# Short-sequence attention: Q and K turned by VectorE 32x32 blocks instead of by TensorE, scores as two accumulating 32-row matmuls, one exp per 2048 columns

## The chip, the cores and the metric

The kernel runs on one core of a Trainium2 chip. The metric is device microseconds for one execution; lower is better. A profiled execution additionally leaves a trace: every instruction of each engine (PE is TensorE's matmuls, PEld its weight loads, DVE is VectorE, ACT ScalarE, POOL GpSimd, SP SyncE) and every DMA packet.

## The reference

For each of 32 x 12 = 384 heads, with 128 positions and a head dimension of 64, all float32 in and out:

```python
def reference(q, k, v):                       # each (32, 12, 128, 64)
    scale = 1.0 / np.sqrt(q.shape[-1])
    scores = scale * np.matmul(q, k.transpose(0, 1, 3, 2))
    scores_max = np.max(scores, axis=-1, keepdims=True)
    attn = np.exp(scores - scores_max)
    attn = attn / (np.sum(attn, axis=-1, keepdims=True) + 1e-8)
    return np.matmul(attn, v).astype(np.float32)
```

The inputs are small (0.1 times a normal draw), so both kernels take the exponential without subtracting the maximum.

## The kernel before

**Layout.** The position index of a head is split as `s = g*4 + t` (32 groups `g` of `T = 4` consecutive positions). One partition row holds one `(head, g)`, so four heads (`A = 4`, index `a`) fill the 128 partitions and make one block; a row then holds 4 x 64 consecutive floats of memory. There are 96 blocks. A chunk is `CB = 4` blocks (16 heads), and there are `NCH = 24` chunks.

**Loads.** All 72 loads (`q_bf`, `k_bf`, `v_bf` of each chunk, L69) are issued by GpSimd at the start, ahead of all compute, and turn float32 into bfloat16 on the way. Every chunk has buffers of its own (`pin`, 24 of them), so no load waits for compute.

**Compute** goes by pairs of blocks (48 pairs, two to a chunk), in three stages that are one pair apart; the order is written out by hand (`manual_schedule`), and each engine works through its list in that order:

- `stage_a`: 16 TensorE transposes of Q and K into `t_ps` (L87), one VectorE copy of the result into `qkt` (L91); 16 matmuls with a slice of the identity that gather V's rows by head into `v_ps` (L98), one ScalarE copy into one of four `v2s` tiles (L103). A column of ones stands beside V there, so that the last product also gives the row sums.
- `stage_b`: 8 matmuls K·Qᵀ (contraction over 64 rows) into `s_ps` (L111), and one exponential of 1024 columns into `attn` (L117).
- `stage_c`: 32 matmuls attn·V into `o_ps` (L130), a reciprocal of the row sums (L140) and a multiplication (L141) on VectorE into `o_sb`; after the second pair of a chunk SyncE stores the chunk (L144).

PSUM is full: `t_ps` and `v_ps` have one buffer each, `s_ps` two, and `o_ps` one. Every TensorE matmul or transpose is two instructions for the engine, a weight load and a matmul; a pair of blocks has 16 + 16 + 8 + 32 = 72 of them, hence 144 instructions, and a chunk 288.

Of the kernel before, what the change touches and what calls it, by code (L numbers as in the profile page):

```python
# [9 lines left out]
@with_exitstack  # L10
def kernel(
    ctx: ExitStack,
    tc: tile.TileContext,
    q: bass.AP,
    k: bass.AP,
    v: bass.AP,
    out: bass.AP,
):


    nc = tc.nc
    f32 = mybir.dt.float32
    bf16 = mybir.dt.bfloat16

    B, H, S, D = q.shape
    assert S == 128 and D == 64
    scale = 1.0 / (D ** 0.5)
    T = 4
    A = 4
    G = S // T  # L30
    NBLK = B * H // A
    CB = 4
    NCH = NBLK // CB
    NG = NBLK // 2
    GPC = CB // 2

    def blocks(x):
        return x.rearrange("b h (g t) d -> (b h g) (t d)", t=T).rearrange(
            "(n p) x -> p n x", p=128)

    qr, kr, vr, orr = blocks(q), blocks(k), blocks(v), blocks(out)

    singles = ctx.enter_context(tc.tile_pool(name="singles", bufs=1))
    pin = ctx.enter_context(tc.tile_pool(name="pin", bufs=NCH))
    pt = ctx.enter_context(tc.tile_pool(name="pt", bufs=3))
    pa = ctx.enter_context(tc.tile_pool(name="pa", bufs=3))
    po = ctx.enter_context(tc.tile_pool(name="po", bufs=4))
    ps_t = ctx.enter_context(tc.tile_pool(name="ps_t", bufs=1, space=bass.MemoryType.PSUM))
    ps_v = ctx.enter_context(tc.tile_pool(name="ps_v", bufs=1, space=bass.MemoryType.PSUM))
    ps_s = ctx.enter_context(tc.tile_pool(name="ps_s", bufs=2, space=bass.MemoryType.PSUM))  # L50
    ps_o = ctx.enter_context(tc.tile_pool(name="ps_o", bufs=1, space=bass.MemoryType.PSUM))

    ident = singles.tile([128, 128], bf16)
    make_identity(nc, ident)
    NV2 = 4
    v2s = []
    for i in range(NV2):
        v2 = singles.tile([128, A, 2, D + 1], bf16, name=f"v2_{i}")
        nc.vector.memset(v2[:, :, :, D:D + 1], 1.0)  # L59
        v2s.append(v2)  # L60

    chunks = {}

    def load(c):
        sl = slice(c * CB, (c + 1) * CB)
        tiles = []
        for src, tag in ((qr, "q_bf"), (kr, "k_bf"), (vr, "v_bf")):
            x = pin.tile([128, CB, T, D], bf16, tag=tag, name=tag)
            nc.gpsimd.dma_start(out=x, in_=src[:, sl, :].rearrange("p n (t d) -> p n t d", t=T))  # L69
            tiles.append(x)  # L70
        chunks[c] = tiles

    for c in range(NCH):
        load(c)

    with tc.manual_schedule():
        qkts, attns, osbs = {}, {}, {}

        def stage_a(i):
            c, r = divmod(i, GPC)  # L80
            q_bf, k_bf, v_bf = chunks[c]
            bs = slice(2 * r, 2 * r + 2)
            t_ps = ps_t.tile([128, T, 2, 128], bf16, tag="t_ps", name="t_ps")
            for t in range(T):
                for j, x in enumerate((q_bf, k_bf)):
                    for b in range(2):
                        nc.tensor.transpose(  # L87
                            t_ps[b * D:(b + 1) * D, t, j, :], x[:, 2 * r + b, t, :], ident,
                            tile_position=(0, b * D))
            qkt = pt.tile([128, 2, A, T, G], bf16, tag="qkt", name="qkt")  # L90
            nc.vector.tensor_copy(  # L91
                qkt.rearrange("p j a t g -> p t (j a) g"),
                t_ps.rearrange("p t j (a g) -> p t (j a) g", a=A))
            qkts[i] = qkt
            v_ps = ps_v.tile([128, A, 2, D], f32, tag="v_ps", name="v_ps")
            for a in range(A):
                for t in range(T):
                    nc.tensor.matmul(  # L98
                        v_ps[t * G:(t + 1) * G, a, :, :],
                        lhsT=ident[:, a * G:(a + 1) * G],  # L100
                        rhs=v_bf[:, bs, t, :],
                        start=True, stop=True, tile_position=(0, t * G))
            nc.scalar.copy(v2s[i % NV2][:, :, :, :D], v_ps)  # L103

        def stage_b(i):
            qkt = qkts.pop(i)
            s_ps = ps_s.tile([128, 2, A, 128], f32, tag="s_ps", name="s_ps")
            for a in range(A):
                for j in range(2):
                    pr = slice(j * D, (j + 1) * D)  # L110
                    nc.tensor.matmul(  # L111
                        s_ps[:, j, a, :],
                        lhsT=qkt[pr, 1, a].rearrange("p t g -> p (t g)"),
                        rhs=qkt[pr, 0, a].rearrange("p t g -> p (t g)"),
                        start=True, stop=True)
            attn = pa.tile([128, 2, A, 128], bf16, tag="attn", name="attn")
            nc.scalar.activation(out=attn, in_=s_ps, func=mybir.ActivationFunctionType.Exp,  # L117
                                 bias=0.0, scale=scale)
            attns[i] = attn

        def stage_c(i):
            c, r = divmod(i, GPC)
            attn = attns.pop(i)
            v2 = v2s[i % NV2]
            o_ps = ps_o.tile([128, 2, 512], f32, tag="o_ps", name="o_ps")
            for j in range(2):
                ov = o_ps[:, j, :T * (D + 1)].rearrange("p (t e) -> p t e", t=T)
                for t in range(T):
                    for a in range(A):
                        nc.tensor.matmul(  # L130
                            ov[a * G:(a + 1) * G, t, :],
                            lhsT=attn[:, j, a, t * G:(t + 1) * G],
                            rhs=v2[:, a, j, :],
                            start=True, stop=True, tile_position=(0, a * G))
            ov = o_ps[:, :, :T * (D + 1)].rearrange("p j (t e) -> p j t e", t=T)
            if r == 0:
                osbs[c] = po.tile([128, CB, T, D], f32, tag="o_sb", name="o_sb")
            o_sb = osbs[c]
            recip = pa.tile([128, 2, T], f32, tag="recip", name="recip")
            nc.vector.reciprocal(recip, ov[:, :, :, D])  # L140
            nc.vector.tensor_mul(o_sb[:, 2 * r:2 * r + 2], ov[:, :, :, :D],  # L141
                                 recip.to_broadcast([128, 2, T, D]))
            if r == GPC - 1:
                nc.sync.dma_start(  # L144
                    out=orr[:, c * CB:(c + 1) * CB, :],
                    in_=o_sb.rearrange("p n t d -> p n (t d)"))
                osbs.pop(c)

        for s in range(NG + 2):
            if s < NG:  # L150
                stage_a(s)
            if 0 <= s - 1 < NG:
                stage_b(s - 1)
            if 0 <= s - 2 < NG:
                stage_c(s - 2)


# [28 lines left out]
```

## Time and profile before

| | |
|---|---|
| median of 3 runs | 168.92 us (168.44 to 169.7) |
| the profiled execution | 168.79 us, of which the trace spans 167.0 us |
| PE busy / PEld busy | 108.6 / 80.4 us |
| VectorE busy / ScalarE busy / GpSimd busy | 74.4 / 76.2 / 54.1 us |
| mean granted TensorE clock | 0.759 of full speed |
| TensorE instructions | 3456 matmuls and 3456 weight loads |
| bytes | 37.75 MB read from HBM, 12.58 MB written |

No engine is busy for much over two thirds of the span, so the busy shares alone don't tell what sets the time. The span has two stages that are read apart: while inputs are being loaded, and after that.

### The profile page before, as it was taken

What the parts mean: (1) busy time and instruction counts of PE and PEld (TensorE: products, weight loads), DVE (VectorE), ACT (ScalarE), POOL (GpSimd) and SP (SyncE); (2) the same over time, 40 slices, a digit from 0 to 9 for tenths busy, and PEclk for the clock granted to TensorE, in tenths of its full rate; (3) what the DMA queues carried; (4) which work ended last, traced back from release to release, by engine and by line L of the source; (5) the groups of instructions that cost most, each with busy time, mean ns of one, the idle gap of its engine ahead of it and who ended that gap; (6) DMA issues with size and microseconds to landing.
All of it is one profiled execution on the core that took longest, in us unless ns stands there. A gap on an engine that the chain in (4) does not pass through costs nothing.

```text
span 167.0 us, 7438 instructions
## 1 busy us (share of the span) xinstructions
PE 108.6 (65%) x3456; PEld 80.4 (48%) x3456; DVE 74.4 (45%) x148; ACT 76.2 (46%) x97; POOL 54.1 (32%) x78
## 2 busy tenths in 40 slices
PE   0279619559558747686796576675595688878730
PEld 0256517446346435454574454454473566656520
DVE  0035515444334453333373351373433377767640
ACT  3027533336253353371544272570362676767730
POOL 7955535343433534444433533534000000000000
PEclk9999995876955895555567855696555899999985
DMA  3999999999999999999999999999999133333333
GB/s 45 141 195 198 192 226 202 237 209 231 231 208 241 197 242 237 201 241 198 223 218 242 218 222 240 197 244 222 214 235 219 46 129 134 129 129 129 129 129 126
DMA packets 50718, 31.93 MB, mean 191 GB/s; under 512 B 1536, under 2 KB 50688, under 8 KB 50688
## 3 DMA queue, kind: packets, MB, share of 16 engines
q0 software_dynamic: 38016, 18.88, 84.3%
q1 hardware_dynamic: 12672, 12.58, 25.3%
q8 instruction: 27, 0.44, 1.0%
q14 instruction: 3, 0.02, 0.0%
HBM read 37.75 MB, written 12.58 MB: 301 GB/s over the span
## 4 chain that ended last, share of the span: by engine, by line
PE 38%; DMA 38%; issue 16%; DVE 3%; POOL 3%; POOLq 0%
DMA k_bf<-in_k_dram 16%; PE t_ps L87 13%; DMA v_bf<-in_v_dram 13%; PE o_ps L130 10%; DMA q_bf<-in_q_dram 9%; PE v_ps L98 8%; PE s_ps L111 7%; DVE o_sb L141 2%; POOL q_bf L69 1%; POOL k_bf L69 1%; DVE qkt L91 1%; DVE recip L140 1%; POOL v_bf L69 0%; POOL ident masks.py:199 0%; POOL ident masks.py:197 0%
## 5 line engine op out<-in xcount | busy, mean ns | idle before, releaser
L103 ACT CAST v<-v_ps 128x512 bf16<-128x512 f32 x48 | 28.2, 587 | 76.9 <-PE v_ps L98 76.7
L117 ACT ACTIVATE attn<-s_ps 128x1024 bf16<-128x1024 f32 x48 | 49.1, 1026 | 6.2 <-PE s_ps L111 6.2
L87 PE MATMUL t_ps<-ident,q_bf 128*64 128x128 bf16 x384 | 38.7, 274 | 7.6 <-DMA q_bf<-in_q_dram 5.1
L87 PE MATMUL t_ps<-ident,k_bf 128*64 128x128 bf16 x384 | 38.4, 271 | 8.0 <-issue 5.9
L130 PE MATMUL o_ps<-v,attn 128*32 128x65 bf16 x1536 | 27.9, 218 | 22.5 <-issue 20.6
L91 DVE COPY qkt<-t_ps 128x1024 bf16<-128x1024 bf16 x48 | 33.0, 687 | 20.6 <-PE t_ps L87 19.7
L140 DVE RECIPROCAL recip<-o_ps 128x8 f32<-128x8 f32 x48 | 10.0, 208 | 65.4 <-PE o_ps L130 64.7
L87 PEld LDWEIGHTS <-q_bf 128*64 128x64 bf16 x384 | 27.1, 139 | 16.5 <-issue 8.1
L130 PEld LDWEIGHTS <-attn 128*32 128x32 bf16 x1536 | 19.4, 110 | 31.3 <-issue 27.9
L141 DVE TENSOR_TENSOR o_sb<-o_ps,recip 128x512 f32<-128x512 f32 x48 | 33.2, 691 | 1.9 <-DVE recip L140 0.3
L98 PE MATMUL v_ps<-v_bf,ident 128*32 128x128 bf16 x768 | 25.3, 263 | 9.5 <-issue 6.4
L87 PEld LDWEIGHTS <-k_bf 128*64 128x64 bf16 x384 | 28.2, 143 | 3.7 <-DMA k_bf<-in_k_dram 2.3
L111 PE MATMUL s_ps<-qkt 64*128 64x128 bf16 x384 | 24.5, 260 | 6.0 <-issue 6.0
L69 POOL DMA_DIRECT2D k_bf<-in_k_dram x24 | 17.9, 746 | 22.2 <-DMA v_bf<-in_v_dram 22.2
L69 POOL DMA_DIRECT2D q_bf<-in_q_dram x24 | 18.0, 752 | 21.2 <-DMA k_bf<-in_k_dram 20.9
L69 POOL DMA_DIRECT2D v_bf<-in_v_dram x24 | 17.9, 745 | 19.0 <-DMA q_bf<-in_q_dram 19.0
L98 PEld LDWEIGHTS <-ident 128*32 128x32 bf16 x768 | 14.2, 111 | 16.7 <-issue 12.0
L111 PEld LDWEIGHTS <-qkt 64*128 64x128 bf16 x384 | 13.7, 110 | 13.5 <-issue 10.8
L103 ACT ACT_TABLE_LOAD x1 | 1.3, 1283 | 0.7 <-PEq L170 0.7
L59 DVE MEMSET v<- 128x8 bf16 x4 | 0.2, 65 | 0.8 <-PEq L170 0.8
masks.py:199 POOL TENSOR_SCALAR_AFFINE_SELECT ident<-ident 128x128 bf16<-128x128 bf16 x1 | 0.3, 304 | 0.1
masks.py:197 POOL MEMSET ident<- 128x128 bf16 x1 | 0.2, 204 | 0.3 <-POOLq L170 0.3
(4 smaller groups left out, 0.4 us busy)
## 6 DMA issues: line engine op xcount, KB each, us to landing
out_dram<-o_sb SPq DMA_DIRECT2D x24, 512.0 KB, 7.6
q_bf<-in_q_dram POOLq DMA_DIRECT2D x24, 256.0 KB, 13.8
k_bf<-in_k_dram POOLq DMA_DIRECT2D x24, 256.0 KB, 13.9
v_bf<-in_v_dram POOLq DMA_DIRECT2D x24, 256.0 KB, 14.0
```

What stands on the lines that cost most here:

```text
L59: nc.vector.memset(v2[:, :, :, D:D + 1], 1.0)
L69: nc.gpsimd.dma_start(out=x, in_=src[:, sl, :].rearrange("p n (t d) -> p n t d", t=T))
L87: nc.tensor.transpose(t_ps[b * D:(b + 1) * D, t, j, :], x[:, 2 * r + b, t, :], ident, tile_position=(0, b * D))
L91: nc.vector.tensor_copy(qkt.rearrange("p j a t g -> p t (j a) g"), t_ps.rearrange("p t j (a g) -> p t (j a) g", a=A))
L98: nc.tensor.matmul(v_ps[t * G:(t + 1) * G, a, :, :], lhsT=ident[:, a * G:(a + 1) * G], rhs=v_bf[:, bs, t, :], start=True, stop=True, tile_ ...
L103: nc.scalar.copy(v2s[i % NV2][:, :, :, :D], v_ps)
L111: nc.tensor.matmul(s_ps[:, j, a, :], lhsT=qkt[pr, 1, a].rearrange("p t g -> p (t g)"), rhs=qkt[pr, 0, a].rearrange("p t g -> p (t g)"), st ...
L117: nc.scalar.activation(out=attn, in_=s_ps, func=mybir.ActivationFunctionType.Exp, bias=0.0, scale=scale)
L130: nc.tensor.matmul(ov[a * G:(a + 1) * G, t, :], lhsT=attn[:, j, a, t * G:(t + 1) * G], rhs=v2[:, a, j, :], start=True, stop=True, tile_pos ...
L140: nc.vector.reciprocal(recip, ov[:, :, :, D])
L141: nc.vector.tensor_mul(o_sb[:, 2 * r:2 * r + 2], ov[:, :, :, :D], recip.to_broadcast([128, 2, T, D]))
```

## The change

TensorE no longer transposes. A VectorE 32x32-block transpose (`turn`, L78) goes from the loaded tile in SBUF to a `qt` or `kt` tile in SBUF, 1024 columns at a time, one for Q and one for K of each chunk. It transposes inside groups of 32 partitions, so head `a` comes to lie on partitions `32a` to `32a+31`, with the 64 features as two groups of 32 (`J = 2`). The scores of a head are thus two matmuls with 32 contraction rows each, accumulated in PSUM, and each head uses a row group of the array of its own (`tile_position=(a * 32, 0)`, L101). The work goes by chunks of four blocks: V's matmuls have 256 columns (L89), the exponential 2048 (L107), V's copy 1024 (L92). PSUM: `s_ps` takes four banks, `v_ps` two, `o_ps` two, one buffer each. `v2s` has three tiles. The loads, the output product, its two VectorE instructions and the store are as before, now in `outputs` and `finish`.

```diff
-    ps_t = ctx.enter_context(tc.tile_pool(name="ps_t", bufs=1, space=bass.MemoryType.PSUM))
+    ps_s = ctx.enter_context(tc.tile_pool(name="ps_s", bufs=1, space=bass.MemoryType.PSUM))
     ps_v = ctx.enter_context(tc.tile_pool(name="ps_v", bufs=1, space=bass.MemoryType.PSUM))
-    ps_s = ctx.enter_context(tc.tile_pool(name="ps_s", bufs=2, space=bass.MemoryType.PSUM))
     ps_o = ctx.enter_context(tc.tile_pool(name="ps_o", bufs=1, space=bass.MemoryType.PSUM))
...
+        def turn(c, which):
+
+            x = chunks[c][which]
+            xt = pt.tile([128, J, CB, T, G], bf16, tag="qk"[which] + "t", name="qk"[which] + "t")
+            nc.vector.transpose(
+                xt.rearrange("p j n t g -> p (n t) j g"),
+                x.rearrange("p n t (j e) -> p (n t) j e", j=J))
+            qts[c, which] = xt
+
+        def values(c):
+
+            v_bf = chunks[c][2]
+            v_ps = ps_v.tile([128, A, CB, D], f32, tag="v_ps", name="v_ps")
             for a in range(A):
                 for t in range(T):
                     nc.tensor.matmul(
-                        v_ps[t * G:(t + 1) * G, a, :, :],
-                        lhsT=ident[:, a * G:(a + 1) * G],
-                        rhs=v_bf[:, bs, t, :],
-                        start=True, stop=True, tile_position=(0, t * G))
-            nc.scalar.copy(v2s[i % NV2][:, :, :, :D], v_ps)
+                        v_ps[t * G:(t + 1) * G, a], lhsT=ident[:, a * G:(a + 1) * G],
+                        rhs=v_bf[:, :, t, :], start=True, stop=True, tile_position=(0, t * G))
+            nc.scalar.copy(v2s[c % NV2][:, :, :, :D], v_ps)
...
+        def scores(c):
+            qt, kt = qts.pop((c, 0)), qts.pop((c, 1))
+            s_ps = ps_s.tile([128, A, CB, 128], f32, tag="s_ps", name="s_ps")
+            for n in range(CB):
+                for j in range(J):
+                    for a in range(A):
+                        pr = slice(a * 32, (a + 1) * 32)
+                        nc.tensor.matmul(
+                            s_ps[:, a, n, :],
+                            lhsT=kt[pr, j, n].rearrange("p t g -> p (t g)"),
+                            rhs=qt[pr, j, n].rearrange("p t g -> p (t g)"),
+                            start=(j == 0), stop=(j == J - 1), tile_position=(a * 32, 0))
+            attn = pa.tile([128, A, CB, 128], bf16, tag="attn", name="attn")
             nc.scalar.activation(out=attn, in_=s_ps, func=mybir.ActivationFunctionType.Exp,
                                  bias=0.0, scale=scale)
-            attns[i] = attn
+            attns[c] = attn
...
+        turn(0, 0)
+        turn(0, 1)
+        values(0)
+        for s in range(NCH + 1):
+            c, p, f = s, s - 1, s + 1
+            if c < NCH:
+                scores(c)
+            o0 = outputs(p, 0) if p >= 0 else None
+            if f < NCH:
+                turn(f, 0)
+            if o0 is not None:
+                finish(p, 0, o0)
+            if f < NCH:
+                values(f)
+                turn(f, 1)
+            if p >= 0:
+                finish(p, 1, outputs(p, 1))
```

How the instructions stand shows best on VectorE. Before, in the steady state, one pair of blocks (`t_ps`, `o_ps` are PSUM tiles; a name behind "waits" is the semaphore, of TensorE, of VectorE itself, or of a store that still reads `o_sb`):

```order
L91 COPY qkt<-t_ps 128x4x8x32 [waits PE_49]
L140 RECIPROCAL recip<-o_ps 128x8 [waits PE_49]
L141 TENSOR_TENSOR o_sb<-o_ps,recip 128x512 [waits DVE_49]
L91 COPY qkt<-t_ps 128x4x8x32 [waits PE_49]
L140 RECIPROCAL recip<-o_ps 128x8 [waits PE_49]
L141 TENSOR_TENSOR o_sb<-o_ps,recip 128x512 [waits DMAHW1_49,DVE_49]
```

A chunk had two such copies out of PSUM, each behind TensorE. Now the same stretch of one chunk on VectorE, where DMASW names the semaphore of a load:

```order
L78 STREAM_TRANSPOSE qt<-q_bf 128x16x2x32 [waits DMASW2_49]
L131 RECIPROCAL recip<-o_ps 128x8 [waits PE_49]
L132 TENSOR_TENSOR o_sb<-o_ps,recip 128x512 [waits DMAHW0_49,DVE_49]
L78 STREAM_TRANSPOSE kt<-k_bf 128x16x2x32 [waits DMASW3_49]
L131 RECIPROCAL recip<-o_ps 128x8 [waits PE_49]
L132 TENSOR_TENSOR o_sb<-o_ps,recip 128x512 [waits DMAHW1_49,DVE_49]
```

VectorE itself now waits for loads: each transpose is for the chunk two after the one whose two finishing instructions stand behind it.

On TensorE, the list of before at the turn from one pair of blocks to the next, where a run of the same pair of rows is cut:

```order
L130 LDWEIGHTS attn [waits DVE_49,Activation_49]
L130 MATMUL o_ps<-v_3_93,attn 32x65 [waits PE_49]
...
L87 LDWEIGHTS q_bf [waits DMASW1_49]
L87 MATMUL t_ps<-ident,q_bf 64x128 [waits DVE_49]
...
L87 LDWEIGHTS k_bf [waits DMASW2_49]
...
L98 LDWEIGHTS ident [waits DMASW3_49]
L98 MATMUL v_ps<-v_bf,ident 32x128 [waits Activation_49]
```

And TensorE's list now, over one chunk:

```order
L101 LDWEIGHTS kt [waits DVE_49]
L101 MATMUL s_ps<-qt,kt 128x128 [waits Activation_49]
...
L120 LDWEIGHTS attn [waits DVE_49]
L120 MATMUL o_ps<-v_0_84,attn 32x65 [waits PE_49]
...
L89 LDWEIGHTS ident [waits DMASW1_49]
L89 MATMUL v_ps<-v_bf,ident 32x256 [waits Activation_49]
...
L120 LDWEIGHTS attn [waits DVE_49]
L120 MATMUL o_ps<-v_0_84,attn 32x65 [waits PE_49]
```

TensorE waits for a load at V's matmuls alone; a chunk has 32 score matmuls, 32 output matmuls, 16 for V and again 32 output matmuls, 224 instructions with their weight loads, where there were 288.

## Rows read from the trace of the kernel before

**Rows 1.** The page: span, and three of its rows in 40 slices of 4.175 us.

```profile
span 167.0 us, 7438 instructions
...
PEclk9999995876955895555567855696555899999985
DMA  3999999999999999999999999999999133333333
GB/s 45 141 195 198 192 226 202 237 209 231 231 208 241 197 242 237 201 241 198 223 218 242 218 222 240 197 244 222 214 235 219 46 129 134 129 129 129 129 129 126
```

**Rows 2.** Waits: engine, line, waited for: us in total, times, longest us.

```profile
PEld L130 <- issue: 27.9, 36, 4.0
...
PE o_ps L130 <- issue: 20.6, 13, 3.8
```

**Rows 3.** Windows from gap to gap on TensorE while loading: busy us (instructions), clock.

```profile
44.30:50.70 6.40, 3.96 (x127) 2.85 (x127) 2.29 (x4) 3.12 (x4) 2.93 (x4) 0.60 1.37 222
...
63.60:70.00 6.40, 4.80 (x127) 3.62 (x127) 3.18 (x6) 2.63 (x3) 2.22 (x3) 0.50 1.36 226
...
sum 63.90, PE 44.19 PEld 32.80 DVE 28.12 ACT 27.08 POOL 26.56; mean PE 4.42 PEld 3.28 DVE 2.81 ACT 2.71 POOL 2.66
```

**Rows 4.** The same after the loads, two windows of five.

```profile
144.10:147.90 3.80, 2.89 (x127) 2.11 (x127) 2.21 (x5) 2.95 (x4) 0.00 (x0) 1.00 0.37 125
147.90:151.85 3.95, 3.32 (x127) 2.52 (x127) 2.99 (x6) 2.53 (x5) 0.00 (x0) 1.00 0.31 104
```

**Rows 5.** DMA queues over the whole span: packets, MB, share of 16 engines.

```profile
q0 software_dynamic: 38016, 18.88, 84.3%
q1 hardware_dynamic: 12672, 12.58, 25.3%
q8 instruction: 27, 0.44, 1.0%
```

**Rows 6.** DMA queue of the loads, 0 to 10 us.

```profile
q0 software_dynamic: 2196, 1.09, 88.9%
```

**Rows 7.** The same, 10 to 20 us, when no store moves yet.

```profile
q0 software_dynamic: 3900, 1.94, 144.0%
```

**Rows 8.** Loads and stores, 20 to 120 us.

```profile
q0 software_dynamic: 29458, 14.63, 108.5%
q1 hardware_dynamic: 7392, 7.34, 26.6%
```

**Rows 9.** Stores issued from 130 us on: how many, KB each, us to landing.

```profile
out_dram<-o_sb SPq DMA_DIRECT2D x8, 512.0 KB, 3.0
```

**Rows 10.** The page's groups: busy us, mean ns of one | idle before, releaser.

```profile
L103 ACT CAST v<-v_ps 128x512 bf16<-128x512 f32 x48 | 28.2, 587 | 76.9 <-PE v_ps L98 76.7
L117 ACT ACTIVATE attn<-s_ps 128x1024 bf16<-128x1024 f32 x48 | 49.1, 1026 | 6.2 <-PE s_ps L111 6.2
...
L91 DVE COPY qkt<-t_ps 128x1024 bf16<-128x1024 bf16 x48 | 33.0, 687 | 20.6 <-PE t_ps L87 19.7
L140 DVE RECIPROCAL recip<-o_ps 128x8 f32<-128x8 f32 x48 | 10.0, 208 | 65.4 <-PE o_ps L130 64.7
...
L141 DVE TENSOR_TENSOR o_sb<-o_ps,recip 128x512 f32<-128x512 f32 x48 | 33.2, 691 | 1.9 <-DVE recip L140 0.3
...
L111 PEld LDWEIGHTS <-qkt 64*128 64x128 bf16 x384 | 13.7, 110 | 13.5 <-issue 10.8
```

**Rows 11.** Timeline around 71 us: start, us, what.

```profile
70.11 0.35 PEld L98 LDWEIGHTS <-ident 128*32 128x32 bf16 x16 [1.85 <-DMA k_bf<-in_k_dram]
...
70.66 0.35 PEld L111 LDWEIGHTS <-qkt 64*128 64x128 bf16 x8 [0.20 <-issue]
...
71.20 0.47 PEld L130 LDWEIGHTS <-attn 128*32 128x32 bf16 x32 [0.20 <-issue]
...
71.89 0.21 DVE L140 RECIPROCAL recip<-o_ps 128x8 f32<-128x8 f32 x1 [2.65 <-PE o_ps L130]
```

**Rows 12.** Timeline, the last multiplication.

```profile
162.49 0.69 DVE L141 TENSOR_TENSOR o_sb<-o_ps,recip 128x512 f32<-128x512 f32 x1
```

**Rows 13.** Waits of GpSimd; the third of three such rows, which sum to 62.1 us.

```profile
POOL v_bf L69 <- DMA q_bf<-in_q_dram: 19.0, 21, 2.1
```

More of the change, by code (lines that the diff above doesn't have):

```diff
@@ L30 @@
     G = S // T
+    J = D // 32
     NBLK = B * H // A
@@ L33 @@
     NCH = NBLK // CB
-    NG = NBLK // 2
-    GPC = CB // 2
     def blocks(x):
@@ L54 @@
     make_identity(nc, ident)
-    NV2 = 4
+    NV2 = 3
     v2s = []
     for i in range(NV2):
-        v2 = singles.tile([128, A, 2, D + 1], bf16, name=f"v2_{i}")
+        v2 = singles.tile([128, A, CB, D + 1], bf16, name=f"v2_{i}")
         nc.vector.memset(v2[:, :, :, D:D + 1], 1.0)
         v2s.append(v2)
[L62 to L71, printed above, removed]
@@ L73 @@
-    for c in range(NCH):
-        load(c)
-    with tc.manual_schedule():
[L77 to L95, printed above, removed]
+    chunks, qts, attns, osbs = {}, {}, {}, {}
@@ new lines, with load @@
+    with tc.manual_schedule():
+        def load(c):
+            sl = slice(c * CB, (c + 1) * CB)
+            tiles = []
+            for src, tag in ((qr, "q_bf"), (kr, "k_bf"), (vr, "v_bf")):
+                x = pin.tile([128, CB, T, D], bf16, tag=tag, name=tag)
+                nc.gpsimd.dma_start(
+                    out=x, in_=src[:, sl, :].rearrange("p n (t d) -> p n t d", t=T))
+                tiles.append(x)
+            chunks[c] = tiles
+        def turn(c, which):
[8 more added lines that the diff above has]
+            v_ps = ps_v.tile([128, A, CB, D], f32, tag="v_ps", name="v_ps")
@@ L98, in stage_a @@
                     nc.tensor.matmul(
-                        v_ps[t * G:(t + 1) * G, a, :, :],
-                        lhsT=ident[:, a * G:(a + 1) * G],
-                        rhs=v_bf[:, bs, t, :],
-                        start=True, stop=True, tile_position=(0, t * G))
-            nc.scalar.copy(v2s[i % NV2][:, :, :, :D], v_ps)
[L105 to L116, printed above, removed]
+                        v_ps[t * G:(t + 1) * G, a], lhsT=ident[:, a * G:(a + 1) * G],
@@ L117, in stage_b, with outputs @@
             nc.scalar.activation(out=attn, in_=s_ps, func=mybir.ActivationFunctionType.Exp,
                                  bias=0.0, scale=scale)
-            attns[i] = attn
[L121 to L124, printed above, removed]
+            attns[c] = attn
+        def outputs(c, half):
+            attn = attns[c]
+            v2 = v2s[c % NV2]
             o_ps = ps_o.tile([128, 2, 512], f32, tag="o_ps", name="o_ps")
-            for j in range(2):
-                ov = o_ps[:, j, :T * (D + 1)].rearrange("p (t e) -> p t e", t=T)
+            for i in range(2):
+                n = 2 * half + i
+                ov = o_ps[:, i, :T * (D + 1)].rearrange("p (t e) -> p t e", t=T)
@@ L130, in stage_c, with finish @@
                         nc.tensor.matmul(
[L131 to L136, printed above, removed]
+                            ov[a * G:(a + 1) * G, t, :], lhsT=attn[:, a, n, t * G:(t + 1) * G],
+                            rhs=v2[:, a, n, :], start=True, stop=True, tile_position=(0, a * G))
+            return o_ps
+        def finish(c, half, o_ps):
+            ov = o_ps[:, :, :T * (D + 1)].rearrange("p i (t e) -> p i t e", t=T)
+            if half == 0:
                 osbs[c] = po.tile([128, CB, T, D], f32, tag="o_sb", name="o_sb")
@@ L147, in stage_c @@
                 osbs.pop(c)
[L149 to L155, printed above, removed]
+        for c in range(NCH):
+            load(c)
+        turn(0, 0)
[15 more added lines that the diff above has]
+                finish(p, 1, outputs(p, 1))
 _INS = ['q', 'k', 'v']
```

4 lines of the change are left out of this document (2 added, 2 removed).

## The prediction

> **What bounds the kernel now.** I read the page's slices first. The row of DMA is at its 9 up to the 31st slice and then drops to 3, with the GB/s row falling from 219 to 46 and 129 [rows 1]: inputs arrive until about 31 x 4.175 = 129.4 us, and the remaining 37.6 us of the span are compute and stores. From 130 us on eight of the 24 stores are still to be issued [rows 9]. So compute trails the loads by a third, although no engine is full.
>
> Next, the price of a byte. With loads alone the queue moved 1.94 MB in 10 us [rows 7], 5.15 us per MB (counted in bfloat16). Over 20 to 120 us it moved 14.63 MB beside 7.34 MB of stores [rows 8]: 14.63 x 5.15 = 75.4 us, which leaves 24.6 us for the stores, 3.35 us per MB. So stores and loads share one budget. All bytes [rows 5] come to 18.88 x 5.15 + 12.58 x 3.35 = 97.2 + 42.1 = 139.4 us, and one chunk to 4.05 + 1.76 = **5.81 us**. This budget alone would let the kernel end near 150.
>
> Why does compute trail it? The waits show TensorE idle for "issue", that is for nothing the profile shows, for 20.6 and 27.9 us at one line alone [rows 2]. The windows from the end of one such gap to the end of the next tell what it is: each has 127 matmuls and 127 weight loads, whichever lines these fall on, and ten of them sum to 63.90 us [rows 3]. The instruction queue moved 27 packets, 0.44 MB in all [rows 5], 16 KB each, and TensorE has 3456 matmuls and as many weight loads: one packet per 256 instructions (a window's last two are in no record). So TensorE is fed **256 instructions per 6.39 us** while loads run, whatever they cost to execute; after the loads a block takes 3.80 to 3.95 us [rows 4]. A chunk of 288 instructions needs 288/256 x 6.39 = 7.19 us, more than the 5.81 us of its DMA; eight chunks after the loads need 8 x 288/256 x 3.87 = 34.8 us, 129.4 + 34.8 = 164.2, where the last multiplication ends at 163.2 [rows 12]. The count explains the time in both stages. TensorE's clock stands at 0.50 to 0.60 in these windows and at 1.00 in those after the loads [rows 3, 4]; but TensorE idles 2.0 us of each 6.39, and where the fetch sets the pace faster work only widens the gap.
>
> [...]
>
> **The change part by part.** *TensorE's list.* A chunk goes from 288 to 224 instructions: 224/256 x 6.39 = **5.59 us** per chunk while loading, now below the DMA's 5.81. This is the term that decides: TensorE no longer falls behind the loads, stores spread over the whole load stage, and almost nothing is left to drain. After the loads, 224/256 x 3.87 = 3.39 us.
>
> *TensorE's work.* Output matmuls are as before, 0.47 us per 32 with 0.20 us at a change of tiling [rows 11]. V's 16 matmuls took 0.35 us at 128 columns, so at most 0.70 at 256. Row groups of 32 aren't in the trace; the nearest is the scores of before, which alternate between two groups of 64 rows: 8 in 0.35 us, 44 ns each at a clock of 0.50 [rows 11]. Lower bound: four groups overlap twice as well, 22 ns x 32 = 0.70 us; upper from that row: 1.41; I take the middle, 1.05 us. Sum with two changes of tiling: 1.05 + 2 x 0.47 + 0.70 + 0.40 = 3.1 us per chunk, well inside 5.59, so it costs nothing until the drain.
>
> *VectorE.* Out go two copies (2 x 0.687), in come two block transposes of 1024 columns, which no row shows. Below: the copy, 0.69 us for as many columns. Above: two multiplications of 512 columns [rows 10], 1.38 us. I take the multiplication's rate without paying its start twice: between 8 and 512 columns VectorE's rows rise from 208 to 691 ns, so 1024 columns are 691 + 512 x 0.96 = 1.18; say 1.2 us. Per chunk VectorE then has 2 x 1.2 + 2 x (0.24 + 0.69), the 0.24 being the reciprocal with its step to the multiplication: **4.3 us**, below 5.81. Each transpose waits for a load with an earlier chunk's finishing queued behind it, and the product of the second half waits for `o_ps` from that; but q, k and v of a chunk land a third of 5.81 apart, and behind the last of them come V's matmuls 0.70, products 0.47, scores 1.25, exponential 1.9: under 5 us with hand-overs, so each chunk is done before the next lands. In the drain 4.3 us per chunk is the slowest rate.
>
> [...]
>
> *ScalarE.* From 512 to 1024 columns its rows rise from 587 to 1026 ns [rows 10], so an exponential of 2048 is 1.90 us and V's copy of 1024 is 1.03: 2.93 per chunk instead of 3.23, off the path. With one `s_ps` buffer, scores and exponential are now serial: 0.20 + 1.05 + 0.25 + 1.90 + 0.1 = 3.5 us per chunk; that fits as well.
>
> *GpSimd* issues the same 72 loads and waits for room in its queue 62.1 us in all [rows 13], 2.6 us per chunk. [...]
>
> *The sum.* In the first 10 us 1.09 MB were loaded [rows 6], 5.6 us of work, so loading starts 4.4 us late. Load end: 4.4 + 97.2 + the stores that get through by then. A chunk's store is issued after V of the second next chunk landed, so some 20.5 of 24: 20.5 x 1.76 = 36.1. That is 137.7 us. Tail: V's matmuls 0.70, products 0.47, scores with the change of tiling 1.25, hand-over 0.25, exponential 1.90, hand-over 0.1, then twice products 0.47 + 0.25 and finishing 0.93, and from the last multiplication to the end 167.0 - 163.2 = 3.8 [rows 1, 12]: 11.8 us. TensorE has some 416 instructions in it, up to two block boundaries at about 0.75 us each (a block needs 3.87 and its work 3.1): 13.3. Together 151.0 us. The margin of 5.59 against 5.81 is thin, so part of a chunk may be behind when the loads end; one whole chunk costs 4.3 in the drain and saves 1.76 of stores ahead, +2.5. I take half, 152.2. The profiled execution of before was 168.79 us with a span of 167.0, 1.8 more, and lies 0.1 from the median. **152.2 + 1.8 = 154.0 us.** A tail without gaps and no lag gives 150.5; one and a half chunks behind, 157.
>
> **The rivals.** *A, VectorE becomes the bound.* If a transpose takes T, VectorE needs 2T + 1.86 per chunk and decides from T = 1.97 us on. Then the end is 24 x (2T + 1.86) + some 15 us for the first loads, the last exponential and the last store, + 1.8: at 2.1 us 162, at 2.25 us no change, and if every element passes twice, T = 2 x 1.2 = 2.4, **177**, slower. [...]
>
> *B, the 32-row score matmuls don't overlap.* From (5.81 - 2.45)/32 = 105 ns per matmul on, scores and exponential set the pace. [...] Against it: 44 ns for 64-row groups.
>
> *C, the instruction queue slows down*, since stores now move all the time beside loads. Its windows of before varied by 0.2 us around 6.4. At 7.0 us a chunk needs 6.13, compute is 20 x 0.32 = 6.4 us late when the loads end, and 152.8 + 6.4 makes **159**, where the drain makes none of it good; at 7.4 us, 166 at most.
>
> *D, the gaps aren't the fetch of instructions* but go with elapsed time, and compute stays at 7.2 us per chunk: **169**, no change.
>
> **How the numbers follow.** Forecast (150 to 157) 0.62; C 0.16; A 0.12, of which 0.05 below break-even; B 0.05; D 0.05. Under 1% can't be told from no change here. Faster by more: 0.62 + 0.16 + 0.05 = 0.83; same 0.05; slower 0.07 + 0.05 = 0.12. The range: from 150, the sum without gaps, to 166, C's far end and the part of A below it; outside are A's rest, B and D, less than 0.2.
>
> **What would show it.** In the changed profile the high DMA row lasts until 135 to 139 us, with no more than four stores issued after. TensorE's "issue" waits shrink to under half of now, and its idle time is put down to the loads of V. A transpose takes about 1.2 us (over 1.97: A), the 32 score matmuls 0.7 to 1.4 us (over 3.4: B). Blocks of 254 TensorE instructions that still lie 6.4 us or more apart with gaps between them, and over four stores after the loads, mean C; gaps at the same times as before, with fewer instructions between them, D.

## The result, and the profile after

The changed kernel takes 154.07 us (median of 4 runs, 153.86 to 154.29) against 168.68 us of the kernel before in the same comparison: a ratio of 0.9129, 95% interval 0.9079 to 0.9178. The forecast was 154.0 us. The profiled execution took 154.2 us, of which the trace spans 152.4.

The page of the changed kernel: span, the same three rows in 40 slices, now of 3.81 us, and the queues of the stores and of instructions (packets, MB, share).

```profile
span 152.4 us, 5803 instructions
...
PEclk9999999999999999955555855568555855555765
DMA  1999999999999999999999999999999999994433
GB/s 24 144 187 196 199 193 224 228 229 244 217 230 243 213 231 245 216 228 246 216 227 225 218 246 234 210 245 228 224 238 228 216 246 236 211 200 150 142 139 141
...
q1 hardware_dynamic: 12672, 12.58, 28.7%
q8 instruction: 21, 0.34, 0.8%
```

Against [rows 1, 5]: the DMA row now stays at 9 up to the 36th slice, to 137 us of 152, where it fell at 129 us of 167. As many bytes are moved, 15 us of the span lie behind the busy stretch instead of 38, and 21 blocks of instructions are fetched instead of 27.

The waits of the changed kernel: engine, line, waited for: us in total, times, longest us.

```profile
PE v_ps L89 <- DMA v_bf<-in_v_dram: 63.0, 23, 10.1
...
DVE recip L131 <- PE o_ps L120: 34.0, 28, 2.2
...
PE o_ps L120 <- issue: 3.2, 5, 1.6
PEld L120 <- issue: 2.7, 4, 1.2
```

The "issue" waits at the output product, 20.6 and 27.9 us in [rows 2], are down to 3.2 and 2.7. TensorE waits for V's loads instead, once in nearly every chunk: compute keeps up with the inputs. The page's groups of the changed kernel (busy us, mean ns of one | idle before, releaser) have the operations that the trace of before did not show.

```profile
L92 ACT CAST v<-v_ps 128x1024 bf16<-128x1024 f32 x24 | 24.4, 1015 | 62.9 <-PE v_ps L89 62.9
L107 ACT ACTIVATE attn<-s_ps 128x2048 bf16<-128x2048 f32 x24 | 45.1, 1877 | 10.0 <-PE s_ps L101 9.9
L78 DVE STREAM_TRANSPOSE qt<-q_bf 128x1024 bf16<-128x1024 bf16 x24 | 29.7, 1238 | 12.1 <-DMA q_bf<-in_q_dram 11.9
```

A block transpose of 1024 columns takes 1.24 us (1.2 forecast, 1.97 was the limit), the exponential 1.88 (1.90), V's copy 1.02 (1.03). The end of the span, from the timeline (start, us, what) of the changed kernel:

```profile
139.70 1.05 PE L89 MATMUL v_ps<-v_bf,ident 128*32 128x256 bf16 x16 [2.53 <-DMA v_bf<-in_v_dram]
...
141.11 0.78 PEld L101 LDWEIGHTS <-kt 32*128 32x128 bf16 x32
141.12 1.04 PE L101 MATMUL s_ps<-qt,kt 32*128 32x128 bf16 x32
...
142.27 1.88 ACT L107 ACTIVATE attn<-s_ps 128x2048 bf16<-128x2048 f32 x1 [0.41 <-PE s_ps L101]
...
147.88 0.69 DVE L132 TENSOR_TENSOR o_sb<-o_ps,recip 128x512 f32<-128x512 f32 x1
```

The last load lets V's matmuls go at 139.70, and 12.7 us later all is over. The 32 score matmuls with 32 rows start within 0.78 us, 24 ns each, where the eight with 64 rows took 44 ns each [rows 11]; the granted clock is 0.50 in both places.

### The profile page after: what moved, and what is told of

Read it like the earlier page. It is cut to its first block, busy times and chain, and to the rows that moved or that the text cites. A ratio compares the mean times of both kernels' runs of the same rounds, so it can differ in the third digit from the quotient of the medians.

```text
span 152.4 us, 5803 instructions
## 1 busy us (share of the span) xinstructions
PE 73.4 (48%) x2688; PEld 53.9 (35%) x2688; DVE 98.2 (64%) x147; ACT 70.5 (46%) x49; POOL 54.2 (36%) x78
## 3 DMA queue, kind: packets, MB, share of 16 engines
q0 software_dynamic: 38016, 18.88, 91.7%
## 4 chain that ended last, share of the span: by engine, by line
DMA 84%; issue 4%; POOL 4%; PE 3%; DVE 2%; POOLq 0%
DMA v_bf<-in_v_dram 39%; DMA q_bf<-in_q_dram 25%; DMA k_bf<-in_k_dram 20%; DVE o_sb L132 2%; PE o_ps L120 2%; POOL k_bf L69 1%; POOL q_bf L69 1%; POOL v_bf L69 1%; PE v_ps L89 1%; PE s_ps L101 1%; DVE recip L131 1%; POOL ident masks.py:199 0%; POOL ident masks.py:197 0%; POOLq masks.py:199 0%; POOLq L184 0%
## 5 line engine op out<-in xcount | busy, mean ns | idle before, releaser
L89 PE MATMUL v_ps<-v_bf,ident 128*32 128x256 bf16 x384 | 23.4, 391 | 65.0 <-DMA v_bf<-in_v_dram 63.0
L92 ACT CAST v<-v_ps 128x1024 bf16<-128x1024 f32 x24 | 24.4, 1015 | 62.9 <-PE v_ps L89 62.9
L107 ACT ACTIVATE attn<-s_ps 128x2048 bf16<-128x2048 f32 x24 | 45.1, 1877 | 10.0 <-PE s_ps L101 9.9
L78 DVE STREAM_TRANSPOSE qt<-q_bf 128x1024 bf16<-128x1024 bf16 x24 | 29.7, 1238 | 12.1 <-DMA q_bf<-in_q_dram 11.9
L89 PEld LDWEIGHTS <-ident 128*32 128x32 bf16 x384 | 10.6, 123 | 73.7 <-DMA v_bf<-in_v_dram 61.5
L120 PE MATMUL o_ps<-v,attn 128*32 128x65 bf16 x1536 | 31.4, 238 | 8.4 <-DVE o_sb L132 4.2
L120 PEld LDWEIGHTS <-attn 128*32 128x32 bf16 x1536 | 25.4, 126 | 16.1 <-DVE o_sb L132 11.1
L78 DVE STREAM_TRANSPOSE kt<-k_bf 128x1024 bf16<-128x1024 bf16 x24 | 29.8, 1240 | 1.7 <-DMA k_bf<-in_k_dram 1.5
L101 PE MATMUL s_ps<-qt,kt 32*128 32x128 bf16 x768 | 25.1, 297 | 0.9 <-issue 0.8
L101 PEld LDWEIGHTS <-kt 32*128 32x128 bf16 x768 | 17.9, 131 | 3.8 <-issue 2.0
```

The source lines that it names most:

```text
L78: nc.vector.transpose(xt.rearrange("p j n t g -> p (n t) j g"), x.rearrange("p n t (j e) -> p (n t) j e", j=J))
L89: nc.tensor.matmul(v_ps[t * G:(t + 1) * G, a], lhsT=ident[:, a * G:(a + 1) * G], rhs=v_bf[:, :, t, :], start=True, stop=True, tile_positio ...
L92: nc.scalar.copy(v2s[c % NV2][:, :, :, :D], v_ps)
L101: nc.tensor.matmul(s_ps[:, a, n, :], lhsT=kt[pr, j, n].rearrange("p t g -> p (t g)"), rhs=qt[pr, j, n].rearrange("p t g -> p (t g)"), star ...
L120: nc.tensor.matmul(ov[a * G:(a + 1) * G, t, :], lhsT=attn[:, a, n, t * G:(t + 1) * G], rhs=v2[:, a, n, :], start=True, stop=True, tile_pos ...
```

## The experiments

Theory: before, TensorE was held by the rate at which its instructions arrive (256 per 6.39 us while loads run), so that 288 instructions per chunk lagged behind 5.81 us of DMA; with 224 they don't, and loads and stores set the pace. Rival: TensorE's work (the transposes, with the copies out of PSUM) held the kernel, and taking it away is the gain. A second rival was that the gaps go with elapsed time and not with instructions (D). Times are medians; ratios are to the kernel before, measured on the same chip.

**Fewer instructions in the kernel before, as many columns.**

```diff
-            for a in range(A):
-                for t in range(T):
-                    nc.tensor.matmul(
-                        v_ps[t * G:(t + 1) * G, a, :, :],
-                        lhsT=ident[:, a * G:(a + 1) * G],
-                        rhs=v_bf[:, bs, t, :],
-                        start=True, stop=True, tile_position=(0, t * G))
+            for t in range(T):
+                nc.tensor.matmul(
+                    v_ps[t * G:(t + 1) * G].rearrange("p a n d -> p (a n d)"),
+                    lhsT=ident[:, t * G:(t + 1) * G],
+                    rhs=v_bf[:, bs].rearrange("p n t d -> p (n t d)"),
+                    start=True, stop=True, tile_position=(0, t * G))
```

> The kernel before with V's 16 matmuls of 128 columns per pair made 4 of 512 columns: as many columns through TensorE, 24 matmuls (48 instructions) fewer per chunk, 240 instead of 288. V's rows are then not gathered by head, so the output is not the reference's. Transposes on TensorE, copies out of PSUM, exponentials, loads and stores stay. Theory (TensorE gets 256 instructions per 6.39 us while loads run): 240/256 x 6.39 = 5.99 us per chunk, just above the DMA's 5.81, so time falls to 156 to 159 us. Rival (TensorE's execution time, or the transposes and their copies, held the kernel): the columns are the same and the transposes stay, so 167 to 169 us.

Measured: 156.01 us (155.4 to 156.19), ratio 0.9272 (0.9225 to 0.9319). Transposes, copies out of PSUM and columns are those of before, and the matmuls are busy for 104.2 us of the span, 108.6 before; 48 instructions fewer per chunk bring 12.4 us of the 14.6 that the whole change brings. The rival of TensorE's work is out: it demanded 167 to 169.

**The instructions put back into the changed kernel**, as matmuls of two columns that nothing reads (`range(2)` is 32 per chunk, `range(4)` 64):

```diff
                             rhs=v2[:, a, n, :], start=True, stop=True, tile_position=(0, a * G))
+                for r in range(2):
+                    for a in range(A):
+                        nc.tensor.matmul(
+                            o_ps[a * G:(a + 1) * G, i, 300:302], lhsT=attn[:, a, n, :G],
+                            rhs=v2[:, a, n, :2], start=True, stop=True, tile_position=(0, a * G))
             return o_ps
```

> The changed kernel with 32 matmuls of two columns more per chunk, into columns of o_ps that nothing reads: 288 instructions per chunk again, some 0.5 us more of TensorE time per chunk. Theory: 288/256 x 6.39 = 7.19 us per chunk, so compute trails the loads as before and the gain is gone: 168 to 172 us, loads done by 128 to 131 us. Rival (what was gained is TensorE's and VectorE's work): 0.5 us fits into the 2 to 3 us for which TensorE waits for V's load in every chunk, so 154 to 156 us.

> The same with 64 such matmuls per chunk: 352 instructions, some 1 us more of TensorE time. Theory: 8.79 us per chunk while loading, 184 to 190 us, slower than the kernel before. Rival: 154 to 157 us.

Measured: 167.02 us (166.57 to 168.8, ten runs), ratio 0.9924 (0.9895 to 0.9953), and 188.79 us (188.47 to 190.06), ratio 1.1242 (1.1178 to 1.1307). The first lies 1 us under the range, the second inside. With 288 instructions per chunk some 13 of the 14.6 us are gone again, although the transposes are on VectorE. Windows of the profile with 288, each from the end of a gap to the end of the next (us, busy of TensorE's matmuls and weight loads with their counts, VectorE, ScalarE, GpSimd, granted clock, DMA share, GB/s):

```profile
39.40:45.59 6.19, 3.08 (x128) 2.20 (x128) 3.98 (x6) 1.88 (x1) 2.23 (x3) 1.00 1.36 225
45.59:52.07 6.48, 2.58 (x130) 2.22 (x130) 2.05 (x3) 2.89 (x2) 2.96 (x4) 1.00 1.36 225
52.07:58.26 6.19, 3.30 (x129) 2.26 (x128) 3.99 (x6) 2.89 (x2) 2.26 (x4) 1.00 1.38 219
```

Again 256 instructions to a window of 6.2 to 6.5 us, as in [rows 3], with wholly different instructions in it. That the windows are also as long as before would by itself fit rival D, gaps that go with elapsed time. Against D stand the windows behind the loads, with as many instructions in 3.80 and 3.95 us [rows 4], and the instruction queue. In the trace of the kernel before, each of the 18 gaps between 18 and 128 us ends 1.2 to 1.6 us after a packet of 16 KB, one block, has come in on that queue; in this run it is 18 gaps and 1.3 to 1.7 us. So D is out as well, and the gaps read as waits for the next block.

TensorE's clock does not set the length of a window. Of the ten windows summed in [rows 3] the one with the highest granted clock, 0.93, is

```profile
57.10:63.60 6.50, 3.10 (x128) 2.38 (x127) 2.99 (x6) 2.10 (x3) 2.91 (x4) 0.93 1.35 225
```

and as long as the next one in [rows 3], at 0.50 with 4.80 us of matmuls. (The 1.00 in the windows of the run with 288 is no evidence for this: V's matmuls take 1.04 us there, as they do at 0.50; see the last section.) The page of the run with 288 has the pattern of before in the DMA row:

```profile
span 167.0 us, 7339 instructions
...
DMA  3999999999999999999999999999999133333333
...
q8 instruction: 27, 0.44, 1.0%
```

and from 130 us on its stores are again eight, as in [rows 9]:

```profile
out_dram<-o_sb SPq DMA_DIRECT2D x8, 512.0 KB, 3.0
```

**More TensorE time in few instructions.**

```diff
+            nc.tensor.matmul(
+                o_ps[:, 0, 262:512], lhsT=ident,
+                rhs=v2[:, 0].rearrange("p n e -> p (n e)")[:, :250], start=True, stop=True)
             return o_ps
```

> The changed kernel with two matmuls of 250 columns and the whole array more per chunk: 4 instructions more (228 per chunk, 5.69 us by the count, below 5.81), but with two more changes of tiling more TensorE time per chunk (about 1 us) than the 32 small ones. Theory: 154 to 156 us. Rival (added time on TensorE is what costs): more than the kernel with 32 small matmuls.

Measured: 155.61 us (154.58 to 156.61), ratio 0.9254 (0.919 to 0.9319). TensorE's matmuls are busy for 84.9 us on its page and for 82.5 us on that of the run with 64 small instructions more, against 73.4 us in the changed kernel. So more work in four instructions per chunk costs about 1%, and less work in 64 costs 13 us: on TensorE it is the count that matters here.

**Fewer instructions still**, by leaving out the second accumulating score matmul, half of the contraction (192 per chunk):

```diff
-                for j in range(J):
+                for j in range(1):
...
-                            start=(j == 0), stop=(j == J - 1), tile_position=(a * 32, 0))
+                            start=(j == 0), stop=True, tile_position=(a * 32, 0))
```

> The changed kernel without the second accumulating score matmul (j = 1), which leaves out half of the contraction: 192 instructions per chunk, 4.79 us by the count, and half of the scores' time. Theory (loads and stores now set the pace, 5.81 us per chunk): only the tail gets shorter, 152 to 154.5 us. Rival (TensorE's instructions still set the pace): 24 x 0.8 = 19 us less, 135 to 140 us.

Measured: 152.77 us (152.49 to 154.07), ratio 0.9107 (0.9046 to 0.9169), not to be told from the changed kernel. From 224 down to 192 per chunk, TensorE's count returns nothing that these times show (154.07 and 152.77 us): something else sets the pace.

**Less to store.** One block of each chunk is stored instead of four, three quarters of the output are left out; then the same with half of the contraction left out as well.

```diff
-                    out=orr[:, c * CB:(c + 1) * CB, :],
-                    in_=o_sb.rearrange("p n t d -> p n (t d)"))
+                    out=orr[:, c * CB:c * CB + 1, :],
+                    in_=o_sb[:, 0:1].rearrange("p n t d -> p n (t d)"))
```

> The changed kernel storing one of the four blocks of each chunk, so three quarters of the output are not written: the DMA's 5.81 us per chunk become 4.05 + 0.44 = 4.49. Theory: TensorE's instructions take the pace over at 5.59 us while loads run, these end near 109 us, then 4.4 us per chunk by VectorE: 141 to 146 us. Rival (stores cost nothing beside the loads): 152 to 155 us.

> Both of these cuts at once (half of the contraction and three quarters of the stores left out). Theory: 4.79 us per chunk by the instruction count beside 4.49 of DMA and 4.4 of VectorE: 129 to 134 us. If the fetch of instructions does not follow the count here, the same as with the quarter of the stores alone.

Measured: 136.28 us (136.12 to 137.54), ratio 0.8128 (0.8081 to 0.8174), and 125.99 us (125.79 to 127.11), ratio 0.7512 (0.747 to 0.7555). Both are under their ranges, by 5 and 3 us, but on the right side of both rivals: stores do cost beside loads, and with most of them out of the way TensorE's list decides again, 10.3 us for 32 instructions per chunk that returned 1.3 us with all stores in place. These 32 are half of the scores' work too, so the second run alone does not tell count from work; the windows of the first do, with 256 instructions to each and the same length whether matmuls are busy for 2.99 or 3.68 us. In the second run V's loads are the longer wait again (TensorE's matmuls wait 25.6 us for them and 11.4 for "issue"; in the first run 14.0 and 24.1). Part of the miss shows in the windows of the run with a quarter of the stores:

```profile
39.16:45.35 6.19, 2.99 (x128) 2.01 (x128) 3.98 (x6) 2.89 (x2) 3.65 (x5) 0.58 1.43 204
...
57.74:63.94 6.20, 3.68 (x129) 2.39 (x128) 3.99 (x6) 4.66 (x3) 3.54 (x5) 0.50 1.41 208
...
sum 49.57, PE 30.27 PEld 19.75 DVE 37.60 ACT 25.67 POOL 24.49; mean PE 3.78 PEld 2.47 DVE 4.70 ACT 3.21 POOL 3.06
```

Eight blocks take 49.57 us, 6.20 each and not 6.39, some 3 us over the 16 blocks of the load stage. Where the rest comes from stays open.

**VectorE made the bound.** Every block transpose is issued twice into the same tile.

```diff
+            nc.vector.transpose(
+                xt.rearrange("p j n t g -> p (n t) j g"),
+                x.rearrange("p n t (j e) -> p (n t) j e", j=J))
             qts[c, which] = xt
```

> The changed kernel with every block transpose issued twice into the same tile: VectorE has 4 x 1.24 + 1.86 = 6.8 us per chunk, over the DMA's 5.81. Rival A's sum with T = 2.48 us: 24 x 6.82 + 15 + 1.8 = 180 us. If VectorE had hidden slack or the transposes overlapped, less; if only the loads set the pace, 154.

Measured: 170.88 us (170.47 to 171.36), ratio 1.0195 (1.016 to 1.023). So the danger of rival A is real: with VectorE as the bound the kernel is 2% slower than before. Its sum was 9 us too high. VectorE's timeline of this run:

```profile
80.70 1.23 DVE L78 STREAM_TRANSPOSE qt<-q_bf 128x1024 bf16<-128x1024 bf16 x1
81.96 1.25 DVE L81 STREAM_TRANSPOSE qt<-q_bf 128x1024 bf16<-128x1024 bf16 x1
83.13 0.17 DVE L134 RECIPROCAL recip<-o_ps 128x8 f32<-128x8 f32 x1
83.34 0.69 DVE L135 TENSOR_TENSOR o_sb<-o_ps,recip 128x512 f32<-128x512 f32 x1
83.94 1.23 DVE L78 STREAM_TRANSPOSE kt<-k_bf 128x1024 bf16<-128x1024 bf16 x1
```

From one pair of transposes to the next are 83.94 - 80.70 = 3.24 us. The expectation has 2.48 + 0.93 = 3.41 for it, and the four rows sum to 3.34: an instruction that waits for nothing starts before the recorded end of the one ahead (83.13 against 81.96 + 1.25). That is 2 x 0.17 per chunk, some 8 of the 9 us over 24 chunks.

**The tail.** Behind the last load four half-chunk products go through the one buffer of `o_ps`, while the banks of `v_ps` and `s_ps` lie free.

```diff
-            o_ps = ps_o.tile([128, 2, 512], f32, tag="o_ps", name="o_ps")
+            if (c, half) == (NCH - 2, 1):
+                o_ps = ps_v.tile([128, A, CB, D], f32, tag="v_ps", name="v_ps")
+                o_ps = o_ps.rearrange("p (i b) n d -> p i (b n d)", i=2)
+            elif (c, half) == (NCH - 1, 1):
+                o_ps = ps_s.tile([128, A, CB, 128], f32, tag="s_ps", name="s_ps")
+                o_ps = o_ps[:, :2].rearrange("p i n s -> p i (n s)")
+            else:
+                o_ps = ps_o.tile([128, 2, 512], f32, tag="o_ps", name="o_ps")
```

> The changed kernel, with the second half of the last two chunks' products in PSUM banks of v_ps and s_ps that are free by then, so that four products behind the last load need not wait for o_ps. The chain after the last exponential loses one step of product and finishing, 1.5 to 2 us: 152 to 153 us. Rival (the last stores or instruction fetches end as late anyway): 154 us.

Measured: 152.05 us (151.87 to 153.12), ratio 0.9063 (0.9018 to 0.9108). Its chip was not the changed kernel's, so both were run together:

> The changed kernel itself once more, on one chip with the next one, to compare the two there: 154 us, 0.91 to 0.92 of the kernel before.

> The kernel with the freed PSUM banks in the tail once more. Theory (one step of product and finishing less behind the last exponential): 1.5 to 2 us under the changed kernel on the same chip. Rival (its earlier lead of 2 us was the chip's): within 0.5 us of it.

Measured: the changed kernel 153.6 us (153.05 to 154.59), ratio 0.9136 (0.9093 to 0.918); with the freed banks 152.19 us (150.83 to 152.99), ratio 0.9045 (0.9 to 0.909). The lead of 1.4 us holds, just, with intervals that do not meet; it is a little under the 1.5 to 2 expected. VectorE's timeline of the latter shows the step that went:

```profile
142.41 0.69 DVE L139 TENSOR_TENSOR o_sb<-o_ps,recip 128x512 f32<-128x512 f32 x1
143.02 0.20 DVE L138 RECIPROCAL recip<-v_ps 128x8 f32<-128x8 f32 x1
```

The second half of chunk 22 follows the first at once, where the changed kernel waits for its product; the last halves of chunk 23 do the same. In these two traces the last multiplication ends 2.3 us earlier (145.73 against 148.06), but the span only 1.6: from there to the end it is 4.6 us and not 3.8, with the store of chunk 22 issued just ahead of the last one.

**The scores of the last chunk ahead of V's matmuls**, on top of the freed banks, so that the last exponential starts earlier:

```diff
+        for f in range(1, NCH + 2):
+            p = f - 2
+            if f < NCH:
+                turn(f, 0)
+            if p >= 0:
+                finish(p, 0, o0)
+            if f < NCH:
+                turn(f, 1)
+            if p >= 0:
+                o1 = outputs(p, 1)
+            if f < NCH:
+                scores(f)
+                values(f)
+            if p >= 0:
+                finish(p, 1, o1)
+            if f - 1 < NCH:
+                o0 = outputs(f - 1, 0)
```

> The kernel with the freed PSUM banks in the tail, and each chunk's scores ahead of V's matmuls on TensorE, so that scores and exponential of the last chunk need not wait for the last load. Theory: between the loads' end and the last multiplication one more step goes, 0.7 to 1.5 us: 150.5 to 151.5 us. Rival (the chain behind the last load is VectorE's finishing work, whatever the order): no less than with the banks alone, 152 us.

Measured: 153.0 us (152.32 to 153.13), ratio 0.9113 (0.9076 to 0.9151). No gain over the freed banks alone. In its timeline the product that borrows `v_ps` stands waiting:

```profile
143.04 1.01 ACT L92 CAST v<-v_ps 128x1024 bf16<-128x1024 f32 x1
144.10 0.63 PE L127 MATMUL v_ps<-v,attn 128*32 128x65 bf16 x32 [1.53 <-ACT v L92]
```

ScalarE copies V of the last chunk only behind the exponential in this order, and the bank comes free only then: the new wait takes the place of the old.

## Why the prediction was right

*The bound before* was read rightly: one block of 256 instructions per 6.39 us. Putting 64 instructions back per chunk gives 167.0 us with the transposes on VectorE, and taking 48 away from the kernel before gives 156.0 with them on TensorE. One reading was off without consequence: the ten windows have granted clocks of 0.50 to 0.93, and not of 0.50 to 0.60. With 288 instructions per chunk, in the kernel before and in the changed one with 64 put back, 1.2 to 4.1 us lie between the starts of two weight loads at each crossing from one block to the next beside loads.

*The bound after* is the DMA's 5.81 us per chunk: fewer instructions return nothing (152.8), fewer stores do (136.3). The price per byte held. In the changed kernel, 20 to 120 us, loads and stores moved

```profile
q0 software_dynamic: 27498, 13.65, 100.7%
q1 hardware_dynamic: 8972, 8.91, 32.4%
```

13.65 x 5.15 = 70.3, and (100 - 70.3)/8.91 = 3.33 us per MB of stores, 3.35 forecast.

*The sum* came out within 0.1 us, partly by luck, since errors cancel. V's last load was there at 139.7, 2.0 us later than the 137.7 forecast: three stores were left at that point and not 3.5, worth 0.9, and 1.1 us are more than the prices give. The trace shows where these prices, taken from full queues, do not hold. At 136 us the queue of the loads has 77 of its 38016 packets left,

```profile
q0 software_dynamic: 77, 0.04, 7.1%
```

the last of which goes at 139.3, and around 137 us the mean busy share of the DMA engines is down to 1 to 3 tenths.

The tail took 12.7 us, 0.6 less than 13.3, but not on the path that the sum has. There the last exponential and two products follow the scores, 5.55 us; in the trace it is four products and their finishing, one after another through the one buffer of `o_ps`, 6.35 us (142.22 to 148.57). The exponential ends at 144.15, and the product that reads it waits for VectorE beyond that:

```profile
145.48 0.43 PE L120 MATMUL o_ps<-v,attn 128*32 128x65 bf16 x32 [1.15 <-DVE o_sb L132]
```

Against these 0.8 us stand the 1.5 for two block boundaries, which do not show: no "issue" piece of the chain behind the last load is over 0.14 us. And the 1.2 us set aside for a lag of half a chunk were not needed.

*The single prices* were near: transpose 1.24 (1.2), exponential and copy within 2%; the 32 score matmuls start within 0.78 us, inside the 0.70 to 1.41 from which 1.05 was taken. VectorE's finishing takes 0.81 us in a row of waiting-free instructions for the forecast 0.93 (83.94 - 83.13 above). That cost nothing here, since VectorE is off the path while loads run, and in the tail, where it waits for each product, it does take 0.93 (142.91 to 143.84); but it is most of why rival A's sum was high when it was tried.

*The rivals.* A did not happen, at 1.24 us per transpose, but was a real danger: doubling the transposes makes the kernel slower than before. B did not happen: 24 ns per matmul, and the limit was 105. C did not: TensorE waited for V's load in 23 of 24 chunks, so it kept up with the DMA's 5.81 us, and a block can have taken 256/224 x 5.81 = 6.64 us at most on average, not 7.0. With 240 instructions per chunk, where stores lie closer together than before, three windows took 6.25 to 6.60 us.

*GpSimd* was not disturbed: beside 48 block transposes its DMA instructions take 747 to 753 ns each in the mean, 745 to 752 before.

## What to carry to other kernels

When no engine is full and the waits say "issue", count instructions between the gaps. Here the count was the same whatever the lines (127 or 128 matmuls and as many weight loads in 6.20 to 6.60 us), and fewer and wider instructions were the remedy: four matmuls in place of 16 with the same columns gave 12.4 us of this change's 14.6, though they leave out the gathering of V's rows by head. Then hold the fetch per chunk against the DMA per chunk: the larger was the bound here, 7.19 us of fetch before and 5.81 us of DMA after, and a margin of 4% between 5.59 and 5.81 was enough.

## What the runs showed of the hardware

- How long a block of 256 TensorE instructions took went with what else the DMA engines did: 6.39 us beside loads and stores, 6.20 with a quarter of the stores, 3.80 to 3.95 after the loads. It did not go with TensorE's clock (6.50 us at a granted 0.93, 6.40 at 0.50, both beside loads and stores). The gaps beside loads ended 1.2 to 1.7 us after the block's packet had come in.
- A granted clock of 1.00 in a profile was not always the speed of the rows. V's 16 matmuls at 40, 76 and 87 us in the changed kernel, and at 74 us with half of the contraction, where the profile has 1.00 throughout (window, its length, busy us of the matmuls and of ScalarE, granted clock, DMA share, GB/s):

```profile
40.18:41.22 1.04, 1.04 (x16) 0.00 (x0) 1.00 1.37 220
75.85:76.89 1.04, 1.04 (x16) 0.00 (x0) 0.50 1.24 265
87.06:87.68 0.62, 0.62 (x16) 0.00 (x0) 1.00 1.42 197
74.43:75.47 1.04, 1.04 (x16) 0.00 (x0) 1.00 1.25 254
```

  The first and the last take the 1.04 us of the second, which has 0.50, under a printed 1.00; the third, also at 1.00, takes 0.62. The clocks of single runs here, 0.62 to 0.76 for the changed kernel and 1.00 with half of the contraction, are therefore not to be compared.
- VectorE's durations overlapped where nothing was waited for: 3.24 us for a sequence whose rows sum to 3.34. The sum of durations was 0.10 us too long there.
- Score matmuls of 32 rows on four row groups came at 24 ns each, those of 64 rows on two groups at 44, both at a granted clock of 0.50.
